# A fused HGRN2 and GLA trunk on one core: slots ordered by time, casts of value jobs held in text order, evictions and weight sums moved in priority

## The chip, the cores and the metric

The kernel runs on one core of a Trainium2 chip. The metric is the device time of one execution in microseconds; the smaller, the better. All tensors are float32.

## The reference

One layer with two mixers in parallel on the same normalised input (1024 tokens, 1024 channels). All features come out of one projection; both mixers are gated linear attention, the HGRN2 one with 8 heads of 128 by 128, the GLA one with 4 heads of 128 keys by 256 values:

```python
h = rms_norm(x, norm_w[l]) * (1.0 + scale[:, None, :]) + shift[:, None, :]
proj = h @ w_in[l]
hq, hf, hi, hz, gq, gk, gv, gz, ga, mg = jnp.split(proj, IN_OFFSETS, axis=-1)
y_h = hgrn2_branch(hq, hf, hi, hz, lb_all[l], hgrn_norm_w[l])
y_g = gla_branch(gq, gk, gv, gz, ga, gla_alpha_w[l], gla_alpha_b[l], gla_norm_w[l])
u_h = y_h @ w_branch[l, 0]
u_g = y_g @ w_branch[l, 1]
mg = jax.nn.sigmoid(mg.reshape(B, T, N_BRANCH, D_MODEL))
merged = mg[:, :, 0] * u_h + mg[:, :, 1] * u_g
x = x + gate[:, None, :] * (merged @ w_out[l])
return rms_norm(x, final_norm_w)
```

Each head computes, token by token, `S_t = diag(alpha_t) S_(t-1) + k_t v_t^T` and `o_t = S_t^T q_t`; the kernel does it in chunks.

## The kernel before

**Products.** A float32 factor is held as a rounded part and a rest: ScalarE casts it (L200), VectorE subtracts the cast from it (L201), both in `split`. Three matmuls (high by high, high by low, low by high) make one product. The large products are moreover done in seven products of halves in place of eight (Strassen's way), so that sums and differences of quarters of the factors have to be built: `make_factor` (L1691) and `v_sums` for the activations and the value weights, `weight_sums` (L1156 to L1162) for the gate and branch weights, which VectorE adds and POOL stores to DRAM for later.

**Stages in time.** The first group (matmuls L375, banks emptied by L351) makes normalised queries and keys of GLA. Value stage 0, from about 110 us, makes GLA's values: `Vstage`, matmuls L1852. Then come features of GLA (`Feat`, L583), value stage 1 (HGRN's values, about 348 to 464 us), the features of the HGRN heads (L583), and the last stages: branches and gates (L1304) and the output product (L1481).

**A value stage** has 14 jobs (`Vjob`): seven products in the order 1, 2, 5, 3, 6, 7, 4, each of two parts of the inner dimension (`kk`). A job is four units, one for each of four PSUM banks; a unit is six matmuls of 128 by 512. After the second part of a product each bank is emptied by `Vstage.after`: ScalarE copies it out for products 1 (L1737), 2, 5, 3 and 4 (L1735), and after 3 writes a snapshot back into the bank (L1755); VectorE combines it with a snapshot after 6 (L1759) and 7 (L1763). POOL stores results as v (L1742). The next product's matmuls on that bank wait for this. `prep` makes a job's splits, `load` its loads.

**Beside the jobs** run side tracks. `Stream.go` lets a job issue a unit and calls `weave`, which counts units and lets the heads' `attention` and the weights' sums go on: each is a generator whose `yield n` says how many units to let pass first. A head multiplies queries and decays (L633 to L637), makes scores (matmuls L641, L672), copies them on ScalarE (L692, L750 to L756), transposes keys (L767, copied by L768), makes states (L787) and outputs (L806, L808). GLA's outputs go through L972, L973, L980 and a norm (L949, L950), are multiplied in L987 and stored as yg by POOL (L877).

**Order.** Each engine works through its instructions in a fixed order. A list scheduler sets it when the kernel is built: it follows the order of the text, lets what it takes to be ready go ahead, and `tc.high_priority(offset=n)` makes an instruction count as standing n instructions further up. `tc.keep_in_program_order` holds instructions so marked in the order of the text among themselves.

**Slots.** Work tiles of 4 KB per partition live in 46 slots of SBUF. `Slots.get` takes the free slot with the smallest key; a tile written into it waits until the last readers of the former one are done, be it an engine or a store. `Slots.free` gives the number of tiles taken so far as the key, plus `behind` where the last reader is a store by DMA; `behind` is 0 until the last stages, then 8.

## Time and profile before

| | |
|---|---|
| time, three runs | 1219.4, 1222.74, 1224.36 us; median 1222.74 |
| profiled execution | 1223.05 us, of it the span 1221.3 us |
| TensorE busy, its mean granted clock | 1172.3 us, 96% of the span; 0.991 |
| VectorE, ScalarE, POOL busy | 848.1, 586.3, 123.4 us |

The span runs from the first to the last instruction. In a row of the timeline stand the start, the duration, engine, line, operation, the tiles written and read, and in brackets how long the engine had idled before and what ended this. A group of equal instructions in a row has its count behind the x. A row of the view of waits names the waiting instruction, what it waited for, then the total time, the number of times and the longest one. PEclk is TensorE's granted clock as a share of full speed.

### The profile page before, as it was taken

The page shows a single profiled execution, that of the slowest core. Times are in us where ns is not written, and L with a number is a line of the kernel's source. Part 1 is how long each engine was busy: PE and PEld are TensorE (multiplying, and loading weights), DVE is VectorE, ACT ScalarE, POOL GpSimd, SP SyncE. Part 2 cuts the span into 40 slices and gives each one's busy share as a digit, 9 for nine tenths or more (in the row PEclk, how much of TensorE's full clock was granted, in tenths as well). Part 3 has the DMA queues.
Part 4 walks back from the last instruction along what each step waited for, and adds up shares of the span by engine and source line. Part 5 has one row for each costly group of instructions (what it writes and reads, how often), then busy time and mean ns, then how long its engine had stood idle before and what let it go on. Part 6 is the DMA issues. An engine that isn't in the chain of part 4 may idle for free.

```text
span 1221.3 us, 20302 instructions
## 1 busy us (share of the span) xinstructions
PE 1172.3 (96%) x8137; PEld 954.2 (78%) x8137; DVE 848.1 (69%) x1270; ACT 586.3 (48%) x859; POOL 123.4 (10%) x256
## 2 busy tenths in 40 slices
PE   7999999999998899899999999999999999999997
PEld 5776767788877778688887888888878888878886
DVE  4745766776564766676877895876454765988994
ACT  5674454643453635243343344356544544544554
POOL 4211101010100012111111000000020000000000
PEclk9999999999999999899999999999999999999999
DMA  9764545384734568652835642234798856434433
GB/s 327 249 222 147 200 138 156 122 289 127 240 106 172 171 197 295 200 170 99 251 110 160 198 120 82 95 114 153 241 327 276 264 159 211 153 104 169 162 102 138
DMA packets 150353, 220.19 MB, mean 180 GB/s; under 512 B 8939, under 2 KB 107297, under 8 KB 150258
## 3 DMA queue, kind: packets, MB, share of 16 engines
q1 hardware_dynamic: 131970, 157.84, 41.5%
q0 software_dynamic: 18240, 61.04, 13.1%
q8 instruction: 64, 1.05, 0.4%
q14 instruction: 31, 0.25, 0.1%
q10 hardware_dynamic: 48, 0.01, 0.0%
HBM read 153.84 MB, written 65.01 MB: 179 GB/s over the span
## 4 chain that ended last, share of the span: by engine, by line
issue 50%; PE 32%; POOL 5%; DMA 5%; DVE 3%; ACT 2%; SPq 0%; POOLq 0%; DVEq 0%; ACTq 0%
PE pd L1304 9%; PE sc_ps L1304 5%; PE pm L1304 5%; PE pd L1852 3%; PE pd L1481 3%; DMA b<-in_w_in_dram 3%; POOL ws L1162 2%; PE sc_ps L1481 2%; PE pm L1481 1%; PE pd L583 1%; DMA v<-b 1%; PE pd L375 1%; POOL yh L877 1%; DVE b L201 1%; DMA b<-in_x_dram 1%
## 5 line engine op out<-in xcount | busy, mean ns | idle before, releaser
L583 PE MATMUL pd<-b,b 128*128 128x512 f32 x1632 | 390.3, 395 | 0.0
L583 PEld LDWEIGHTS pd<-b,b 128*128 128x128 f32 x1632 | 302.5, 188 | 64.6 <-issue 0.7
L201 DVE TENSOR_TENSOR b<-b,b 128x1024 fp32r<-128x1024 f32 (+1 forms) x114 | 129.6, 1148 | 78.3 <-ACT b L200 52.0
L1852 PE MATMUL pd<-b,b 128*128 128x512 f32 x672 | 167.7, 404 | 12.1 <-ACT b L1735 4.1
L1304 PE MATMUL pd<-b,b 128*128 128x512 f32 x720 | 173.0, 391 | 0.9 <-DVE b L1396 0.4
L200 ACT CAST b<-b 128x1024 fp32r<-128x1024 f32 (+1 forms) x114 | 111.0, 989 | 123.4 <-DMA b<-in_w_in_dram 39.3
L1852 PEld LDWEIGHTS pd<-b,b 128*128 128x128 f32 x672 | 125.7, 191 | 45.5 <-ACT b L1735 5.9
L1304 PEld LDWEIGHTS pd<-b,b 128*128 128x128 f32 x720 | 134.0, 188 | 31.2 <-DVE b L1396 0.9
L1247 DVE TENSOR_TENSOR b<-b,b 128x1024 fp32r<-128x1024 f32 x56 | 68.2, 1222 | 69.1 <-ACT b L1246 49.1
L1246 ACT CAST b<-b 128x1024 fp32r<-128x1024 f32 x56 | 58.6, 1051 | 68.1 <-PE pm L1304 19.4
L1304 PE MATMUL sc_ps<-b,b 128*128 128x512 f32 x324 | 78.6, 390 | 0.0
L1304 PE MATMUL pm<-b,b 128*128 128x512 f32 x300 | 72.1, 389 | 0.0
L1304 PEld LDWEIGHTS sc_ps<-b,b 128*128 128x128 f32 x324 | 60.4, 188 | 13.3 <-ACT b L1276 0.4
L1224 DVE TENSOR_TENSOR b<-b,b 128x1024 fp32r<-128x1024 f32 x48 | 57.8, 1220 | 16.9 <-ACT b L1223 11.2
L1223 ACT CAST b<-b 128x1024 fp32r<-128x1024 f32 x48 | 49.8, 1050 | 39.9 <-PE pd L1304 15.9
L1304 PEld LDWEIGHTS pm<-b,b 128*128 128x128 f32 x300 | 56.3, 188 | 11.7
L1162 POOL DMA_DIRECT2D ws<-b x64 | 34.7, 542 | 216.4 <-DVE b L1156 83.9
L375 PE MATMUL pd<-b,b 128*128 128x512 f32 x192 | 52.3, 405 | 3.6 <-DVE b L351 2.7
L692 ACT COPY xb<-b 128x512 f32<-128x512 f32 x48 | 29.4, 619 | 43.5 <-PE sc_ps L672 27.3
L375 PEld LDWEIGHTS pd<-b,b 128*128 128x128 f32 x192 | 34.4, 188 | 16.2 <-DVE b L351 3.5
L806 PE MATMUL pm<-scT,b 128*128 128x128 f32 x256 | 46.8, 275 | 0.0
L808 PE MATMUL pm<-b,b 128*128 128x128 f32 x224 | 43.3, 275 | 0.0
(313 smaller groups left out, 1627.4 us busy)
## 6 DMA issues: line engine op xcount, KB each, us to landing
b<-in_w_in_dram SPq DMA_DIRECT2D x72, 512.0 KB, 4.8
ws<-b POOLq DMA_DIRECT2D x64, 256.0 KB, 3.4
b<-ws SPq DMA_DIRECT2D x32, 512.0 KB, 4.8
b<-in_x_dram SPq DMA_DIRECT2D x16, 512.0 KB, 5.9
b<-in_ada_w_dram SPq DMA_DIRECT2D x32, 256.0 KB, 6.4
v<-b POOLq DMA_DIRECT2D x32, 256.0 KB, 3.1
b<-v SPq DMA_DIRECT2D x16, 512.0 KB, 4.6
b<-fx SPq DMA_DIRECT2D x16, 512.0 KB, 4.1
```

What stands on the lines that cost most here:

```text
L200: nc.scalar.copy(hi, src)
L201: nc.vector.tensor_sub(lo, src, hi.bitcast(F32))
L375: nc.tensor.matmul(accs[f], wg(a, d, f), b[d][:, half * 512:half * 512 + 512], start=(d == 0 and n == 0), stop=(d == KT - 1 and n == 2))
L583: nc.tensor.matmul(ps[0:w, th * 512:(th + 1) * 512], a[:, k, 0:w], b[:, th * 512:(th + 1) * 512], start=(k == 0 and n == 0), stop=(k == KT ...
L1162: nc.gpsimd.dma_start(w_sums[b][i // 2][q][:, i % 2 * 512:i % 2 * 512 + 512], parts[p].rearrange("p k f -> p (k f)"))
L1223: nc.scalar.copy(hi, src)
L1224: nc.vector.tensor_sub(lo, src, hi.bitcast(F32))
L1246: nc.scalar.copy(hi, t)
L1247: nc.vector.tensor_sub(lo, t, hi.bitcast(F32))
L1304: nc.tensor.matmul(o, a[:, sl], c, start=(p in (1, 5) and kt == 0 and n == 0), stop=(kt == 3 and n == 2), skip_group_check=True)
L1481: nc.tensor.matmul(o, a, b, start=(p in (1, 5) and kt == 0 and n == 0), stop=(kt == 3 and n == 2), skip_group_check=True)
L1852: nc.tensor.matmul(st.bank[i], x_, w_, start=(p in (1, 5) and kk == 0 and a == 0 and n == 0), stop=(kk == 1 and a == 1 and n == 2), skip_g ...
```

## The change

- `Slots`: the key of a freed slot is the number of units issued so far (`S.now`, from `weave`; plus 2 for each run of the output product), and `behind` is 4 from the start to the end.
- `pinned_split` is used by the value jobs: its casts keep the order of the text.
- `Vstage.after` runs with an offset of 300 (`EVICT_FIRST`), the four adds of `weight_sums` with one of −400 (`BEHIND`).
- `Stream.go` loads up to two jobs more at the start of a job whose `more` is set, and prepares one job less at its unit 0.
- Head 0's query and key are loaded at the start of job 10 of value stage 0, and no longer at job 12.
- In `attention`, the wait after the score copies is 3 units (was 3.5), the one behind the transposes 2.5 (was 1.5).

```diff
--- before.py
+++ after.py
@@ -25,6 +25,7 @@
 C_HQ, C_HF, C_HI, C_HZ = 0, 1024, 2048, 3072
 C_GQ, C_GK, C_GV, C_GZ, C_GA, C_MG = 4096, 4608, 5120, 6144, 7168, 7184
 N_SLOTS = 46
+EVICT_FIRST, BEHIND = 300, -400
 PACE, PACE_H = 1.08, 1.15
 
 
@@ -39,7 +40,8 @@
     def __init__(self, pool, n):
         self.pool = pool
         self.free_list = [(-1, i - n, i) for i in range(n)]
-        self.freed = self.behind = 0
+        self.freed = self.now = 0
+        self.behind = 4
         self.owner = {}
         self.serial = 0
 
@@ -53,7 +55,7 @@
     def free(self, *tiles, sent=False):
         for t in tiles:
             self.freed += 1
-            heapq.heappush(self.free_list, (self.serial + (self.behind if sent else 0), self.freed, self.owner.pop(id(t))[0]))
+            heapq.heappush(self.free_list, (self.now + (self.behind if sent else 0), self.freed, self.owner.pop(id(t))[0]))
 
 
 class Halves:
@@ -198,6 +200,12 @@
             hi = S.get(list(src.shape[1:]), F32R)
             lo = S.get(list(src.shape[1:]), F32R)
         nc.scalar.copy(hi, src)
+        nc.vector.tensor_sub(lo, src, hi.bitcast(F32))
+        return hi, lo
+
+    def pinned_split(src):
+        hi, lo = S.get([2, 512], F32R), S.get([2, 512], F32R)
+        tc.keep_in_program_order(nc.scalar.copy(hi, src))
         nc.vector.tensor_sub(lo, src, hi.bitcast(F32))
         return hi, lo
 
@@ -755,7 +763,7 @@
         for j in range(4):
             nc.scalar.copy(scT[32 * j:32 * j + 32, :, 32 * j:32 * j + 32], blk[32 * j:32 * j + 32])
         scoring.discard(me)
-        yield 3.5
+        yield 3
 
 
         kT = S.get([NCH, P])
@@ -767,7 +775,7 @@
                 nc.tensor.transpose(pt[:, i * P:(i + 1) * P], k[:, ch * P:(ch + 1) * P], ident)
             nc.scalar.copy(kT[:, g * 4:g * 4 + nt, :].rearrange("p c s -> p (c s)"), pt[:, 0:nt * P])
         S.free(k)
-        yield 1.5
+        yield 2.5
         per = 512 // V
         spp = 1024 // V
         st = [S.get([1024]) for _ in range((7 + spp - 1) // spp)]
@@ -842,16 +850,17 @@
         def go(self, loads=2, preps=1):
             n = len(self.jobs)
             for i, job in enumerate(self.jobs):
-                self.ahead(i, loads, 0)
+                self.ahead(i, loads + 2 * job.more, 0)
                 for u, _ in enumerate(job.run()):
                     if job.calls(u):
-                        self.ahead(i, loads + 2 * job.more, preps + job.more)
+                        self.ahead(i, loads + 2 * job.more, preps + (job.more if u else 0))
                     if (n - i, u) in self.hooks:
                         self.hooks[n - i, u]()
                     self.weave(1)
 
         def weave(self, units):
             self.units += units
+            S.now = self.units
             for track in (self.side, self.back):
                 if not track:
                     continue
@@ -1153,11 +1162,13 @@
         s1, s2 = S.get([2, 4, P]), S.get([2, 4, P])
         parts = {5: s1[:, 0], 6: s1[:, 1], 3: s2[:, 0], 7: s2[:, 1]}
         add = nc.vector.tensor_add
-        add(parts[7], x1[:, :, 0], x1[:, :, 1])
-        add(parts[5], x1[:, :, 1], x2[:, :, 1])
+        with tc.high_priority(offset=BEHIND):
+            add(parts[7], x1[:, :, 0], x1[:, :, 1])
+            add(parts[5], x1[:, :, 1], x2[:, :, 1])
         yield 1.5
-        add(parts[6], parts[7], x2[:, :, 1])
-        add(parts[3], parts[6], x2[:, :, 0])
+        with tc.high_priority(offset=BEHIND):
+            add(parts[6], parts[7], x2[:, :, 1])
+            add(parts[3], parts[6], x2[:, :, 0])
         for p, q in SUMS.items():
             nc.gpsimd.dma_start(w_sums[b][i // 2][q][:, i % 2 * 512:i % 2 * 512 + 512],
                                 parts[p].rearrange("p k f -> p (k f)"))
@@ -1563,6 +1574,7 @@
         for p in OUT_PRODUCTS:
             for i in range(4):
                 out_run(p, i)
+                S.now += 2
                 out_after(p, i)
                 for f in at.get((4, p, i), ()):
                     f()
@@ -1799,10 +1811,10 @@
             s, p, kk = self.stage.s, self.p, self.kk
             add = nc.vector.tensor_add
             if s:
-                self.w = split(self.w_raw)
+                self.w = pinned_split(self.w_raw)
                 S.free(self.w_raw)
                 if p not in RAW_X:
-                    self.x = split(self.x_raw)
+                    self.x = pinned_split(self.x_raw)
                     S.free(self.x_raw)
                 return
             if p == 2:
@@ -1815,7 +1827,7 @@
                 add(wq[0, 1][kk], wq[0, 0][kk], wq[1, 1][kk])
                 nc.vector.scalar_tensor_tensor(wq[1, 0][kk], wq[0, 1][kk], -1.0, wq[1, 0][kk], ALU.mult, ALU.subtract)
             raw = wq[W_AT[p]][kk]
-            self.w = split(raw)
+            self.w = pinned_split(raw)
             if p in (3, 6, 7, 4):
                 S.free(raw)
             if p == 3:
@@ -1826,7 +1838,7 @@
                 S.free(xq["22"][kk], sent=True)
             if p not in RAW_X:
                 x = xq[QUAD[p]][kk]
-                self.x = split(x)
+                self.x = pinned_split(x)
                 if p in (7, 4):
                     S.free(x, sent=True)
 
@@ -1852,7 +1864,8 @@
                         nc.tensor.matmul(st.bank[i], x_, w_, start=(p in (1, 5) and kk == 0 and a == 0 and n == 0),
                                          stop=(kk == 1 and a == 1 and n == 2), skip_group_check=True)
                 if kk:
-                    st.after(p, i)
+                    with tc.high_priority(offset=EVICT_FIRST):
+                        st.after(p, i)
                 yield
             S.free(*self.w)
             if p not in RAW_X:
@@ -1864,9 +1877,9 @@
     vjobs = [[Vjob(st, p, kk) for p in PRODUCTS for kk in range(2)] for st in (Vstage(0), Vstage(1))]
 
     def first_head():
-        load_qk(0)
         start_side(gla_attention(0))
 
+    vjobs[0][10].begins = lambda: load_qk(0)
     vjobs[0][12].begins = first_head
 
     def pause(on):
@@ -1910,7 +1923,6 @@
     front()
     stream.go()
     S.free(*h_hi, *h_lo)
-    S.behind = 8
     lent = [dtile() for _ in range(2)]
     R.lend([pd[:, i * 512:i * 512 + 512] for pd in lent[::-1] for i in range(2)])
     last_stages()
```

The new lines move the numbers: what is L201 in `split` is L203 there, L1735 is L1747, L1759 is L1771, L1763 is L1775, L633 to L637 are L641 to L645, L972 is L981; the cast and the subtract of `pinned_split` are L208 and L209. The names b_n are numbered work tiles, pd_n PSUM banks, xb the buffer of a head's multiplied queries.

**VectorE, end of value stage 0**, between the last row that combines product 6 (L1759) and the first that empties a bank after product 7 (L1763); L634 is the first step of GLA head 0. Before:

```order
L1759 SCALAR_TENSOR_TENSOR b_1421<-pd_1129,b_1421 128x512
L201 TENSOR_TENSOR b_1565<-b_1325,b_1564 128x1024
L634 TENSOR_TENSOR xb<-b_1592,b_862 128x32x8
L635 TENSOR_TENSOR xb<-b_1592,b_862 128x32x8x2
L201 TENSOR_TENSOR b_1561<-b_1141,b_1560 128x1024
L636 TENSOR_TENSOR xb<-xb,b_862 128x32x16
L201 TENSOR_TENSOR b_1605<-b_1522,b_1604 128x1024
L1763 TENSOR_TENSOR b_1322<-pd_1128,b_1322 128x512
L637 TENSOR_TENSOR xb<-xb,b_862 128x32x8
```

and with the change:

```order
L1771 SCALAR_TENSOR_TENSOR b_1421<-pd_1137,b_1421 128x512
L209 TENSOR_TENSOR b_1541<-b_1132,b_1540 128x1024
L209 TENSOR_TENSOR b_1545<-b_1316,b_1544 128x1024
L643 TENSOR_TENSOR xb<-b_1518,b_862 128x32x8x2
L209 TENSOR_TENSOR b_1581<-b_1133,b_1580 128x1024
L209 TENSOR_TENSOR b_1585<-b_1317,b_1584 128x1024
L644 TENSOR_TENSOR xb<-xb,b_862 128x32x16
L203 TENSOR_TENSOR b_1622<-b_1516,b_1621 128x1024
L1775 TENSOR_TENSOR b_1326<-pd_1136,b_1326 128x512
L1775 TENSOR_TENSOR b_1349<-pd_1137,b_1349 128x512
```

Between the two stood three subtracts, now there are five; L634 (now L642) has gone ahead of the last L1759, and the second eviction follows the first one directly.

**ScalarE, value stage 1, end of product 5**: L972 reads outputs of a GLA head, L633 starts the next head, L1735 copies a bank out. Before:

```order
L972 ACTIVATE b_3319<-pm_3311 128x512
L633 COPY xb<-b_3351 128x32x32
L972 ACTIVATE b_3319<-pm_3322 128x512
L200 CAST b_3366<-b_3238 128x1024
L200 CAST b_3377<-b_3274 128x1024
L200 CAST b_3417<-b_3303 128x1024
L1735 COPY b_3360<-pd_3001 128x512 x2
L1735 COPY b_3387<-pd_3002 128x512
```

and with the change:

```order
L981 ACTIVATE b_3321<-pm_3313 128x512
L981 ACTIVATE b_3321<-pm_3324 128x512
L208 CAST b_3341<-b_3175 128x1024
L202 CAST b_3373<-b_3274 128x1024
L1747 COPY b_3361<-pd_3007 128x512
L641 COPY xb<-b_3363 128x32x32
L1747 COPY b_3361<-pd_3007 128x512
L1747 COPY b_3383<-pd_3008 128x512
```

The second L972 of the pair came after L633 and is now ahead of it; three casts stood ahead of the first L1735, two do now, and L633 has gone behind it.

**ScalarE, ahead of the first HGRN head**, whose decay comes from L1061 and L1062 (now L1070 and L1071); the casts of b_4263 and b_4385 are those of two feature weights. Before (the two rows that follow are L1061 and L1062):

```order
L200 CAST b_4486<-b_4263 128x1024
L200 CAST b_4026<-b_3930 128x1024
L951 ACT_TABLE_LOAD
L951 ACTIVATE b_3970<-pm_4036,eps_t 128x512
L951 ACTIVATE b_3970<-pm_4040,eps_t 128x512
L200 CAST b_4348<-b_4146 128x1024
L952 ACT_TABLE_LOAD
L952 ACTIVATE b_3970<-b_3970 128x1024
L937 ACT_TABLE_LOAD
L937 ACTIVATE b_4065<-pd_3984 128x1024
L633 COPY xb<-b_4065 128x32x32
L200 CAST b_4611<-b_4385 128x1024
```

and with the change:

```order
L961 ACTIVATE b_3977<-b_3977 128x1024
L946 ACT_TABLE_LOAD
L946 ACTIVATE b_4065<-pd_3962 128x1024
L641 COPY xb<-b_4065 128x32x32
L202 CAST b_4486<-b_4263 128x1024
L202 CAST b_4609<-b_4385 128x1024
L1070 ACTIVATE b_4139<-pd_4068 128x1024
L1071 ACTIVATE b_4140<-pd_4068 128x1024
L673 COPY xb<-b_4065 128x64x4
```

The cast of b_4263 stood far up, ahead of the norm's L951, and now stands with that of b_4385 directly ahead of the decay.

## The prediction

> **What bounds the kernel now.** I read the totals first, then what TensorE waited for, then the granted clock around its longest waits, then the rows of the engines that it waited for.
>
> ```profile
> core 0: 1221.3 us, clock 0.991
> PE 1172.3 (96%) x8137; PEld 954.2 (78%) x8137; DVE 848.1 (69%) x1270; ACT 586.3 (48%) x859; POOL 123.4 (10%) x256
> ```
>
> TensorE is the bound. The change takes no matmul away, so it can only gain idle TensorE time (1221.3 − 1172.3 = 49 us), and matmuls that ran at a lower clock. The view of waits, TensorE's alone, says who ended that idle time (total, times, longest, in us):
>
> ```profile
> PE sc_ps L641 <- DVE xb L637: 5.8, 1, 5.8
> PE pm L787 <- ACT b L768: 5.5, 6, 1.3
> PE pd L1852 <- ACT b L1735: 4.1, 3, 3.7
> PE pd L1852 <- DVE b L1763: 2.9, 1, 2.9
> PE pd L375 <- DVE b L351: 2.7, 2, 1.5
> PE pd L1852 <- ACT b L1737: 1.7, 2, 1.5
> PE pd L1852 <- DVE b L1759: 1.7, 1, 1.7
> PE pd L1852 <- ACT pd L1755: 1.4, 1, 1.4
> PE pm L950 <- DVE b L201: 1.3, 1, 1.3
> ```
>
> The rows of L1852 are a value stage's matmuls that wait until a PSUM bank has been emptied: 4.1 + 2.9 + 1.7 + 1.7 + 1.4 = 11.8 us. The others wait for a step of an attention head, of the GLA norm, or of the first group. Three waits are long (5.8, 3.7, 2.9 us), and behind each of them the windows show the clock down (window, length, busy us by engine, then PEclk):
>
> ```profile
> 182.80:190.00 7.20, 7.17 (x41) 5.33 (x42) 5.96 (x9) 0.00 (x0) 1.63 (x3) 0.57 0.29 109
> 396.90:402.00 5.10, 5.04 (x15) 4.02 (x16) 4.29 (x7) 2.23 (x4) 0.00 (x0) 0.67 0.30 103
> 506.30:512.00 5.70, 5.70 (x76) 4.88 (x77) 5.70 (x11) 1.96 (x3) 1.23 (x3) 0.69 0.37 141
> 426.60:432.00 5.40, 4.39 (x111) 3.42 (x112) 5.40 (x15) 1.86 (x3) 0.94 (x2) 1.00 0.33 106
> ```
>
> Lost clock is (1 − PEclk) times the length: 7.2 × 0.43 = 3.1, 5.1 × 0.33 = 1.7, 5.7 × 0.31 = 1.8 us. The last row follows the 1.7 us wait, and its clock is full: short waits cost only themselves, long ones 1.7 to 3.1 us more.
>
> The Trainium skill ("TensorE: Matmul & The Clock Gate", Part 1 and "Why this matters for your kernels") has the clock fall after an idle window of about 3.4 us and tells to avoid gaps above some 3 us. The 2.89 us gap here was followed by 0.57; the measurement decides. By the page's figure alone that gap would carry no clock loss, and place A below would be an estimated 3.1 us smaller.
>
> **Part by part.** No instruction of a compute engine is added. The edits cost what their new order costs; I go through the places where TensorE waits now.
>
> *A, 182.83 us (value stage 0, product 7 to 4).*
>
> ```profile
> 172.04 0.68 DVE L1759 SCALAR_TENSOR_TENSOR b<-pd,b 128x512 f32<-128x512 f32 x1
> 173.10 1.23 DVE L201 TENSOR_TENSOR b<-b,b 128x1024 fp32r<-128x1024 f32 x1 [0.38 <-ACT b L200]
> 176.56 0.66 DVE L634 TENSOR_TENSOR xb<-b,b 128x256 f32<-128x256 f32 x1 [2.23 <-DMA b<-qk]
> 179.05 1.22 DVE L201 TENSOR_TENSOR b<-b,b 128x1024 fp32r<-128x1024 f32 x1 [1.07 <-DMA v<-b]
> 182.08 0.69 DVE L1763 TENSOR_TENSOR b<-pd,b 128x512 f32<-128x512 f32 x1
> 182.83 1.65 PE L1852 MATMUL pd<-b,b 128*128 128x512 f32 x3 [2.89 <-DVE b L1763]
> ```
>
> VectorE is in order: L1763, which frees the bank, stood behind L634, which waited 2.23 us for head 0's query load, and behind a subtract L201 that waited 1.07 us for a store out of its slot. The query load now starts two jobs earlier, and slots just stored are taken four units later, so I strike both waits. But the order puts two more L201 ahead of L1763 (five instead of three after the last L1759; L634 now stands earlier). From 172.04 to the end of L1763 (182.08 + 0.69) are 10.7 us, of which 0.38 + 2.23 + 1.07 = 3.7 are waits and 7.0 work. Less 0.6 for L634 and plus two L201 of 1.2 less a little overlap, that is 8.7, so L1763 ends near 180.7. TensorE ran dry at 182.83 − 2.89 = 179.94: 0.8 us stay. Gain 2.1, and 3.1 of clock: **5.2**. If the loads don't come earlier, the two L201 make it worse by 2.3.
>
> *B, 396.96 us (value stage 1, product 5 to 3).*
>
> ```profile
> 386.67 6.55 PE L1852 MATMUL pd<-b,b 128*128 128x512 f32 x28
> 388.76 1.23 DVE L201 TENSOR_TENSOR b<-b,b 128x1024 fp32r<-128x1024 f32 x1 [6.86 <-DMA v<-b]
> 388.06 1.05 ACT L633 COPY xb<-b 128x1024 f32<-128x1024 f32 x1 [2.61 <-DMA b<-qk]
> 394.29 2.13 ACT L200 CAST b<-b 128x1024 fp32r<-128x1024 f32 x2 [3.75 <-issue]
> 396.33 0.58 ACT L1735 COPY b<-pd 128x512 f32<-128x512 f32 x1
> ```
>
> L201 waited 6.86 us for a store of v; behind it stood L973 and L980 (the gated GLA sum), whose result the first of the two casts at 394.29 needs, and behind these ScalarE's L1735. In the new order all L972 stand together ahead of L633, L980 comes before the subtracts, and L1735 follows one cast after it, with L633 behind. ScalarE is free at 388.06 − 2.61 = 385.5; one L972, the last L973 and L980, two casts and L1735 take about 0.6 + 0.7 + 1.2 + 2.1 + 0.6 = 5.2: it ends near 390.7, against 393.2, where TensorE ran dry. The wait goes: 3.7 + 1.7 = **5.4**, with 2.5 us to spare.
>
> *C, the short waits of value stage 1.*
>
> ```profile
> 360.54 1.64 ACT L756 COPY scT<-blk 32x256 f32<-32x256 f32 x4
> 362.20 1.09 ACT L1737 ACTIVATE b<-pd 128x512 f32<-128x512 f32 x2
> 411.88 1.04 ACT L200 CAST b<-b 128x1024 fp32r<-128x1024 f32 x1
> 412.83 0.59 ACT L1755 COPY pd<-b 128x512 f32<-128x512 f32 x1
> ```
>
> L1737 stood behind a head's score copies, L1755 behind a cast, L1759 behind score steps of the same kind. All three now stand further ahead. L1755 gains the cast (0.95 of 1.4 us), L1737 and L1759 most of 1.5 and 1.7. What is put back are score steps of a head, each 0.2 to 1 us: TensorE's next score matmuls come that much later, so I take 3.5 of 4.6: **3.5**.
>
> *D, 506.30 us (first HGRN head).*
>
> ```profile
> SPq L565 <- DMA yg<-b: 10.6, 1, 10.6
> 491.82 0.37 SPq L565 DMA_DIRECT2D b<-in_w_in_dram  x1
> 477.20 23.32 PE L583 MATMUL pd<-b,b 128*128 128x512 f32 x102
> 497.60 1.05 ACT L200 CAST b<-b 128x1024 fp32r<-128x1024 f32 x1 [10.06 <-DMA b<-in_w_in_dram]
> 499.47 1.02 ACT L1062 ACTIVATE b<-pd 128x1024 f32<-128x1024 f32 x1
> 505.52 0.64 DVE L637 TENSOR_TENSOR xb<-xb,b 128x256 f32<-128x256 f32 x1
> ```
>
> A weight load was held 10.6 us on SP, because its slot was still being stored as yg; its cast stood 10.06 us on ScalarE, ahead of L1061 and L1062, which the head's first scores need. TensorE was dry from 500.5. In the new order that load gets a slot that no store reads. Yet the cast ahead of it, formerly done by 480, now has a slot of yg, so ScalarE still waits for this store, until about 491.6 (the old load was issued at 491.82, when it landed) or, if the gate sums ahead of L987 wait for their own, earlier queued loads, up to 1.5 us longer. Two casts, L1061 and L1062 take 4 us; the two adds L1156 and L1157 that stood between L634 and L637 (0.6 each) are gone. From L1062 on 505.52 + 0.64 − 499.47 = 6.7 us remain, less 1.2. L1062 starts near 494.7 to 496.2, L637 ends near 500.2 to 501.7. I take 501.7, a rest of 1.2: gain 4.6 + 1.8 = **6.4**.
>
> *E, the end of the first group*: a loss.
>
> ```profile
> 111.16 1.23 DVE L1691 TENSOR_TENSOR b<-b,b 128x1024 f32<-128x1024 f32 x1 [1.03 <-DMA b<-h]
> ```
>
> L1691 and a subtract come ahead of two L351, which free banks of the first group. One such row more in the way is 1.2 us; the casts that wait for these L1691 come earlier instead. I book **−0.8**, between +0 and −2.4 with the clock kept.
>
> *F, the rest.* L950 waited 1.3 us for L201, with a subtract and an add ahead that the new order puts behind: **1.3**. Of the six waits of L787, two heads' follow an add that waited for its load ahead of the score steps; the row of one is
>
> ```profile
> 659.82 0.75 DVE L1033 TENSOR_SCALAR b<-b,cs 128x1024 f32<-128x1024 f32 x1 [2.48 <-DMA b<-in_ada_w_dram]
> ```
>
> In those two heads the add has moved: **2.3** for both. The other yields move L767 six matmuls up and leave L787 in place: nothing, since L787 waits for L768, which stands behind ScalarE's score copies. Behind 850 us the engines' orders agree: nothing.
>
> Sum of gains: 5.2 + 5.4 + 3.5 + 6.4 − 0.8 + 1.3 + 2.3 = 23.3 us. Against it stand **new waits**: nearly every tile has another slot, and SP's loads of the weights' sums have changed places. Nothing in the trace prices these; bounds are 0 and two long waits of A's kind, 2 × (2.9 + 3.1) = 12. Short waits are the commoner row, so I take three of 1.5: 4.5. The profiled execution took 1223.05 us (1.75 around the span), 0.3 above the median of 1222.74. 1223.05 − 23.3 + 4.5 = 1204.3, less 0.3 for the median: **1204 us**.
>
> **The rivals.**
>
> *1. Everything works and no new wait comes.* 1222.74 − 23.3 = 1199; with the other L787 waits (3.2 us) gone too, 1196. For it: B has 2.5 us to spare. Against it: A and D are close to their limits.
>
> *2. The waits move.* What was behind the evictions gets late instead. One long wait with its clock loss stays or appears (A or D: 5 to 6 us), C gains half: 1204 + 6 + 2 = 1212, and with a second one 1218. For it: at A five L201 stand where three did, and at D a yg slot is still in the way.
>
> *3. The orders barely change what is waited for.* The offsets move only instructions whose neighbours are within 300 or 400 of text, and DVE's rows for GLA heads read alike in both orders. Then only B's reorder counts and E takes back some: 1219 to 1223.
>
> *4. Slower: pinned casts hold ScalarE.* A cast kept in text order waits for its own load with all evictions behind it.
>
> ```profile
> ACT b L200 <- DMA b<-in_w_in_dram: 39.3, 9, 10.1
> ```
>
> Casts already wait 39.3 us for weight loads, up to 10.1 at once. If a value stage's products meet this, each costs what B costs now, 5.4 us. With D and F still gained (10) and A, B, C lost, three such waits make 1222.7 − 10 + 16.2 = 1229: from three on the change is slower. Against it: a stage's loads run at least two ahead, so most casts have their data.
>
> The store's landing decides much in all of these.
>
> ```profile
> v<-b POOLq DMA_DIRECT2D x32, 256.0 KB, 3.1
> ```
>
> A unit is six matmuls, 6 × 6.55 / 28 = 1.4 us, so four units are 5.6 us against a landing of 3.1: late only where POOL itself is. The Trainium skill ("SBUF — State Buffer", section "SBUF: two separate sides") lets VectorE's two-port work starve the descriptors of POOL's transfers, which speaks against slots that wait for stores while VectorE is made busier. With VectorE busy 69% the row shows 3.1 us at the median, so it bears out no such starving here; by the rule a store can stretch by a VectorE instruction, an estimated 1 us, within the four units.
>
> **How the numbers follow.** Forecast (1199 to 1211) 0.55; rival 1 0.12; rival 2 0.18, half of it above 1216.6; rival 3 0.08; rival 4 0.07. A measurement of this kernel tells about 0.5%, 6.1 us, from no change: faster is below 1216.6, slower above 1228.9. Faster: 0.55 + 0.12 + 0.09 = 0.76, with one point of rival 3 0.77; same 0.16; slower 0.07. Leaving out the better part of rival 1, and rivals 3 and 4, the range is 1196 to 1219.
>
> **What would show it.** Right: no TensorE wait for L1735 or L1763 above 1.5 us, the clock 1.00 at 182 to 190 and 397 to 402, the wait of L641 under 2 us, two waits of L787 fewer, and a span near 1202. A: L634 without a wait for qk; B: no L201 waiting for v for 6 us; D: the cast ahead of L1061 starting before 495. Wrong: a TensorE wait over 2.9 us for L351 near 108, or at a place that has none now; or ScalarE's L200 waiting for weight loads in the value stages.

## The result, and the profile after

The changed kernel takes 1217.3 us at the median (eight runs, 1211.31 to 1218.46) against 1222.67 us for the kernel before (eight runs beside it, 1219.4 to 1224.36): a ratio of 0.9955, 95% interval 0.994 to 0.9969. The change is 5.4 us faster, a quarter to a third of the 18.7 us that were forecast: inside the stated range, outside the likeliest case's own. It is also less than the 0.5% (6.1 us) that the prediction took for what a measurement tells from no change; with eight runs of each the interval still leaves 1 out.

In the text below, a line that the prediction calls L633 to L637 is L641 to L645 now, L787 is L795, L768 is L776, L351 and L375 are L359 and L383, L1691 is L1703, L891 and L897 are L900 and L906, L1735, L1759, L1763 and L1852 are L1747, L1771, L1775 and L1864, L1061 is L1070, and the casts and subtracts L200 and L201 are L202 and L203, or L208 and L209 where they are held.

The totals of the changed kernel's page (the profiled execution took 1218.36 us):

```profile
core 0: 1216.7 us, clock 0.988
PE 1173.9 (96%) x8137; PEld 956.0 (79%) x8137; DVE 846.7 (70%) x1270; ACT 584.0 (48%) x859; POOL 122.9 (10%) x256
```

TensorE idles 42.8 us (1216.7 − 1173.9), 6.2 us less than before, but it is busy 1.6 us longer with the same 8137 matmuls, and its mean clock is lower: 0.988 for 0.991 (the eight runs go from 0.987 to 0.993). So in this execution some of the idle time that went was paid back at a lower clock. TensorE's waits (total in us, times, longest; left out are those of the first 25 us, which every kernel here has, up to 3.5 us long, and most of the short ones):

```profile
PE pm L795 <- ACT b L776: 9.2, 5, 5.2
PE pd L383 <- DVE b L359: 5.2, 1, 5.2
PE sc_ps L649 <- DVE xb L645: 4.8, 1, 4.8
PE pm L775 <- ACT b L922: 2.7, 1, 2.7
PE pd L1864 <- ACT b L1747: 1.7, 4, 1.1
PE pd L1864 <- ACT b L1749: 0.9, 2, 0.6
PE pd L1864 <- DVE b L1771: 0.3, 1, 0.3
```

The value stages' waits for banks are 1.7 + 0.9 + 0.3 = 2.9 us, where they were 11.8. But four waits of 2.7 to 5.2 us stand where before there were three: one in the first group (at 113 us), one at a GLA head's transposes (221 us), the old one at the first HGRN head (494 us), and one at a head's states (660 us). The windows behind these four, and one at place B in value stage 1 (window, length, busy us by engine, then PEclk):

```profile
113.10:121.00 7.90, 7.89 (x22) 5.66 (x23) 5.72 (x7) 2.24 (x3) 2.71 (x5) 0.68 0.45 168
220.80:228.00 7.20, 7.14 (x27) 6.03 (x28) 4.64 (x7) 7.11 (x9) 0.00 (x0) 0.78 0.00 0
494.20:502.00 7.80, 7.73 (x80) 6.47 (x81) 7.66 (x14) 1.95 (x3) 0.00 (x0) 0.60 0.25 69
660.10:668.00 7.90, 7.83 (x34) 6.99 (x35) 4.24 (x11) 1.69 (x4) 1.62 (x3) 0.74 0.39 111
395.00:402.00 7.00, 6.38 (x27) 5.08 (x28) 6.07 (x9) 6.94 (x10) 0.00 (x0) 1.00 0.40 150
```

Lost clock in this execution, worked out as in the prediction, is 7.9 × 0.32 + 7.2 × 0.22 + 7.8 × 0.40 + 7.9 × 0.26 = 2.5 + 1.6 + 3.1 + 2.1 = 9.3 us; the three places of before lost 6.6. At B the clock is full.

Where the time went is seen best by the **lead**: how much earlier the trace of after has done the same amount of matmul work than that of before (where the matmuls stand in one order, how much earlier the same matmul starts). Its changes from place to place add up to the 4.6 us between the two spans:

| stretch | lead at its end, us | change | forecast |
|---|---|---|---|
| to 93 us | 0.7 | +0.7 | 0 |
| first group's end (E) | −4.4 | −5.1 | −0.8 |
| value stage 0 (A) | 1.2 | +5.6 | 5.2 |
| transposes at 221 us | 0 | −1.2 | 0 |
| value stage 1 (B and C) | 9.5 | +9.5 | 8.9 |
| GLA norm at 476 us (L950) | 11.1 | +1.6 | 1.3 |
| first HGRN head (D) | 10.8 | −0.3 | 6.4 |
| HGRN heads to 629 us | 9.6 | −1.2 | 0 |
| heads at 664 to 694 us | 4.0 | −5.6 | 1.2 (half of F) |
| heads to 782 us | 6.6 | +2.6 | 1.2 (half of F) |
| the rest | 4.6 | −2.0 | 0 |

The value stages gave what was forecast and a little more. The loss lies at E, D and 660 us, and a smaller one at 221 us. The rows of the timeline there (start, duration, engine, line, tiles; in brackets the idle time before) show these three causes. At E, VectorE and TensorE:

```profile
103.35 1.23 DVE L1703 TENSOR_TENSOR b<-b,b 128x1024 f32<-128x1024 f32 x1 [4.14 <-DMA h<-b]
...
110.09 1.23 DVE L906 TENSOR_TENSOR b<-b,b 128x1024 f32<-128x1024 f32 x1 [3.64 <-ACT b L904]
...
113.11 1.65 PE L383 MATMUL pd<-b,b 128*128 128x512 f32 x3 [5.23 <-DVE b L359]
```

The difference L1703 writes over a tile that POOL stores as h. The store was issued at 94.72 us and took 8.5 us to land (issue to landing), and L1703, which was ordered ahead of the key's normalisation, waited for it with VectorE standing still. Behind it came L900, L901, ScalarE's answer, L906 (3.5 us later than the L897 of before, at 106.56), and only then the L359 that frees the bank. At D, the store of yg, the casts behind it on ScalarE, and the end of the chain on VectorE:

```profile
477.27 2.13 POOL L886 DMA_DIRECT2D yg<-b  x4
...
484.18 2.00 ACT L202 CAST b<-b 128x1024 fp32r<-128x1024 f32 x2 [5.75 <-DMA yg<-b]
...
493.49 0.64 DVE L645 TENSOR_TENSOR xb<-xb,b 128x256 f32<-128x256 f32 x1
```

TensorE was dry here from 494.3 − 4.8 = 489.5 us on, 11 us earlier than before (500.5). The casts began once the store had landed, at 484.2, and only some 7.5 us earlier than that landing before (about 491.8, when the load that waited for it was issued). And at 660 us, on ScalarE:

```profile
653.31 2.00 ACT L202 CAST b<-b 128x1024 fp32r<-128x1024 f32 x2 [7.25 <-DMA ws<-b]
...
659.53 0.97 ACT L776 COPY b<-pm 128x512 f32<-128x512 f32 x2
```

The casts of a later feature's weight stand ahead of what the running head needs, up to the copy of its transposed keys (L776), and wait 7.25 us for a slot out of which a weights' sum is still being stored.

### The profile page after: what moved, and what is told of

It is laid out like the page before. It is cut to its first block, busy times and chain, and to the rows that moved or that the text cites. A ratio compares the mean times of both kernels' runs of the same rounds, so it can differ in the third digit from the quotient of the medians.

```text
span 1216.7 us, 20300 instructions
## 1 busy us (share of the span) xinstructions
PE 1173.9 (96%) x8137; PEld 956.0 (79%) x8137; DVE 846.7 (70%) x1270; ACT 584.0 (48%) x859; POOL 122.9 (10%) x256
## 4 chain that ended last, share of the span: by engine, by line
PE 48%; issue 35%; DMA 5%; DVE 4%; POOL 4%; ACT 2%; SPq 1%; POOLq 0%; DVEq 0%; ACTq 0%
PE pd L1315 10%; PE pd L591 8%; PE pd L1864 8%; PE pm L1315 5%; PE sc_ps L1315 5%; PE pd L1492 3%; DMA b<-in_ada_w_dram 2%; POOL ws L1173 2%; PE pd L383 2%; PE sc_ps L1492 2%; PE pm L1492 1%; DVE b L209 1%; PE pm L814 1%; PE sc_ps L383 1%; PE pm L816 1%
## 5 line engine op out<-in xcount | busy, mean ns | idle before, releaser
L1864 PE MATMUL pd<-b,b 128*128 128x512 f32 x672 | 164.1, 398 | 3.0 <-ACT b L1747 1.7
L1864 PEld LDWEIGHTS pd<-b,b 128*128 128x128 f32 x672 | 123.8, 188 | 36.9 <-ACT b L1747 4.9
L1258 DVE TENSOR_TENSOR b<-b,b 128x1024 fp32r<-128x1024 f32 x56 | 68.3, 1223 | 69.8 <-ACT b L1257 56.9
L202 ACT CAST b<-b 128x1024 fp32r<-128x1024 f32 (+1 forms) x70 | 65.9, 951 | 80.0 <-DMA b<-in_w_in_dram 22.9
L203 DVE TENSOR_TENSOR b<-b,b 128x1024 fp32r<-128x1024 f32 (+1 forms) x70 | 76.7, 1101 | 36.7 <-ACT b L202 35.8
L1257 ACT CAST b<-b 128x1024 fp32r<-128x1024 f32 x56 | 58.4, 1049 | 66.3 <-PE pm L1315 17.6
L209 DVE TENSOR_TENSOR b<-b,b 128x1024 fp32r<-128x1024 f32 x44 | 52.7, 1225 | 35.8 <-ACT b L208 34.2
L1235 DVE TENSOR_TENSOR b<-b,b 128x1024 fp32r<-128x1024 f32 x48 | 57.8, 1222 | 19.7 <-ACT b L1234 13.9
L1234 ACT CAST b<-b 128x1024 fp32r<-128x1024 f32 x48 | 49.7, 1049 | 44.9 <-PE pd L1315 15.5
L700 ACT COPY xb<-b 128x512 f32<-128x512 f32 x48 | 29.2, 619 | 62.4 <-PE sc_ps L680 36.4
L383 PE MATMUL pd<-b,b 128*128 128x512 f32 x192 | 52.8, 408 | 6.0 <-DVE b L359 5.2
L383 PEld LDWEIGHTS pd<-b,b 128*128 128x128 f32 x192 | 34.8, 190 | 18.7 <-DVE b L359 6.1
L208 ACT CAST b<-b 128x1024 fp32r<-128x1024 f32 x44 | 44.3, 1050 | 6.8 <-PE pd L1864 3.5
```

The costliest lines, as they stand in the source:

```text
L202: nc.scalar.copy(hi, src)
L203: nc.vector.tensor_sub(lo, src, hi.bitcast(F32))
L209: nc.vector.tensor_sub(lo, src, hi.bitcast(F32))
L383: nc.tensor.matmul(accs[f], wg(a, d, f), b[d][:, half * 512:half * 512 + 512], start=(d == 0 and n == 0), stop=(d == KT - 1 and n == 2))
L1235: nc.vector.tensor_sub(lo, src, hi.bitcast(F32))
L1257: nc.scalar.copy(hi, t)
```

## The experiments

Each ratio is against runs of the kernel before on the same chip, whose median went from 1218.35 to 1222.67 us between chips; so ratios are compared, not times. Two theories stood at the start. **Theory one:** the gain in the value stages comes from the changed slots and the earlier query load, as forecast, and what is lost comes from equal keys in the front stage (E), the offset of the weights' sums (660 us) and the two yields (221 us). **Theory two:** the held casts and the evictions' offset make the gain, and the slots are of no use or do harm.

| kernel | edit | ratio [95%] | its median; before beside it |
|---|---|---|---|
| after_again | the change, once more | 0.996 [0.9941, 0.9978] | 1216.79; 1220.59 |
| before_again | the kernel before, once more | 0.9995 [0.9986, 1.0005] | 1220.18; 1220.18 |
| u_evict | no offset for evictions | 0.9993 [0.9979, 1.0006] | 1218.42; 1219.35 |
| u_behind | no offset for sums | 0.9976 [0.9963, 0.9989] | 1215.88; 1219.35 |
| u_yields | old yields | 0.9958 [0.9941, 0.9974] | 1213.91; 1219.35 |
| u_slots | slot keys as before | 0.993 [0.99, 0.9959] | 1213.36; 1220.59 |
| u_pin | value casts not held | 1.0038 [1.0017, 1.0059] | 1227.37; 1220.59 |
| u_ahead | `Stream.go` as before | 0.9999 [0.9985, 1.0013] | 1220.62; 1220.44 |
| u_qk | query load at job 12 | 0.9986 [0.9974, 0.9998] | 1218.67; 1220.18 |
| f_front | old keys in the front stage only | 0.9964 [0.9948, 0.9981] | 1213.71; 1219.35 |
| x_allpin | feature casts held too | 0.9924 [0.9907, 0.9941] | 1210.35; 1218.35 |
| c_fy | f_front and old yields | 0.9916 [0.9884, 0.9948] | 1212.53; 1220.59 |
| c_fyp | c_fy, feature casts held | 0.9945 [0.9931, 0.996] | 1212.56; 1218.35 |
| c_syp | old keys, old yields, feature casts held | 0.9897 [0.988, 0.9915] | 1206.83; 1218.35 |
| c_sypb | c_syp, no offset for sums | 0.9882 [0.9867, 0.9897] | 1205.19; 1220.18 |
| pin_alone | before, value casts held | 1.0043 [1.0027, 1.0058] | 1223.89; 1218.35 |
| pin_qk | pin_alone, query load at job 10 | 1.0024 [1.0011, 1.0037] | 1222.74; 1220.18 |
| b_allpin | pin_qk, feature casts held | 0.9935 [0.9913, 0.9956] | 1213.53; 1220.44 |

### Both kernels once more

> The changed kernel as it is, on the same chip as the runs beside it, as their base line. A ratio of 0.9955 to the kernel before was measured for it; the same is expected here, within 0.002.

> The kernel before as it is, for a trace of it on the chip of these runs: the ratio is 1 within 0.002. Expected: the same three long waits as in the trace read for the prediction (183, 397 and 506 us); if one of them is below 1.5 us here, the chips differ in it and what the change gained there is less than the first trace says.

The second trace of the change has the same four waits (4.5, 2.7, 4.4 and 4.7 us), that of the kernel before the same three (2.1, 3.5 and 5.9). The waits belong to the kernels, not to one execution. The clock behind them doesn't: at A in the second trace of the kernel before, the clock was 0.75 over 6.7 us, a loss of 1.7 us where the first one lost 3.1.

### The front stage's keys (E)

```diff
-    heapq.heappush(self.free_list, (self.now + (self.behind if sent else 0), ...
+    key = self.serial - 10000 if self.front else self.now + (self.behind if sent else 0)
+    heapq.heappush(self.free_list, (key, ...
...
     front()
+    S.front = False
```

> The changed kernel, but until the front stage ends a freed slot's key is the number of tiles taken (as before the change), since no unit is counted there and all keys are equal; after it, the change's keys. My theory: equal keys gave the activation loads of value stage 0 their slots 20 us earlier, so the differences were put ahead of the gate's steps on VectorE and held them 4.1 us: the 5.2 us wait near 113 us with 2.5 us of clock. With this edit that place is as before (1.2 + 1.5 us, full clock): 1211 to 1213 us, unless the other slots of stage 0 bring new waits. Rival, the earlier preparation of jobs did it: the 5.2 us stay, 1217.

While the front stage runs, no unit is counted, so all its freed slots have the key 0 or 4; here they have the number of tiles taken, as before. VectorE at E, and TensorE's waits, in this kernel (its lines are two further down):

```profile
101.13 0.69 DVE L902 TENSOR_SCALAR b<-b 128x1024 f32<-128x1024 f32 x1 [4.44 <-ACT b L900]
...
106.74 1.23 DVE L908 TENSOR_TENSOR b<-b,b 128x1024 f32<-128x1024 f32 x1 [3.65 <-ACT b L906]
```

```profile
PE pm L797 <- ACT b L778: 8.7, 5, 5.1
PE sc_ps L651 <- DVE xb L647: 5.0, 1, 5.0
PE pd L385 <- DVE b L361: 2.8, 2, 1.8
```

L906's counterpart is back at 106.7 us, the wait for L361 at 1.8. With the old keys the loads of h wait for their slots until 108 us (86.4 in the change); so the differences are not ready early, and the scheduler leaves them behind the normalisation. The cause of E is shown. But the gain does not stay in this trace. Its lead over that of after_again is some 4 us at 123 us, 3.2 at 183 and at 483, 1.9 at 543, 0.3 at 723 and 0 at the end. Most of it goes at the first HGRN head and at 660 us. These are the windows of f_front, then those of after_again:

```profile
491.80:499.80 8.00, 7.99 (x81) 6.67 (x82) 7.83 (x15) 1.95 (x3) 0.00 (x0) 0.62 0.24 68
656.80:664.80 8.00, 7.94 (x32) 7.00 (x33) 4.01 (x10) 1.42 (x4) 1.63 (x3) 0.69 0.39 112
```

```profile
494.40:502.40 8.00, 7.94 (x87) 6.70 (x88) 7.83 (x15) 1.96 (x3) 0.00 (x0) 0.79 0.24 68
658.70:666.70 8.00, 8.00 (x39) 7.28 (x40) 4.79 (x11) 2.17 (x3) 1.62 (x3) 0.79 0.41 122
```

At the first head the wait is 0.6 us longer than in after_again (5.0 for 4.4), and the lost clock 1.4 us more (8.0 × 0.38 against 8.0 × 0.21); at 660 us it is 0.4 and 0.8. So the larger part went to the clock, and that this is the edit's doing is not shown: the last section has waits of equal length with very different losses. The traced execution (1216.1 us) is also the second slowest of six, whose median is 1213.71. Still, by the ratios (0.9964 for 0.9955 and 0.996) this edit gains nothing that can be told.

### The yields (221 us)

```diff
-        yield 3
+        yield 3.5
...
-        yield 2.5
+        yield 1.5
```

> The changed kernel with the two waits of attention as before (3.5 units behind the score copies, 1.5 behind the transposes). My theory: the transposes that come six matmuls earlier run into ScalarE's copies, which caused the 2.7 us wait near 221 us (2.2 before, in two pieces without a lower clock); with the old waits 1.3 + 0.9 come back in place of 2.7 + 1.6 of clock: 1214 to 1216 us. Rival, the split of the gate's matmuls beside it did it: the 2.7 us stay, 1217.

The wait at the transposes is back at its old size, and the clock behind it is full:

```profile
PE pm L775 <- ACT b L922: 1.3, 1, 1.3
```

```profile
220.80:228.00 7.20, 5.14 (x23) 4.09 (x24) 6.20 (x10) 7.09 (x9) 0.00 (x0) 1.00 0.11 31
```

The transposes six matmuls earlier came into ScalarE's score copies, behind which stands the L922 that frees their bank. This trace leads that of after_again by 2.15 us at its end, but the median ratio is that of the change: about 2 us in one execution, none that the runs can tell. The long wait at 660 us is not in this trace either (0.2 us there); one of 2.5 us stands at 611 us in its place, with a clock of 0.72 over the 6.2 us behind it.

### The wait at 660 us

```diff
-EVICT_FIRST, BEHIND = 300, -400
+EVICT_FIRST, BEHIND = 300, 0
```

> The changed kernel with BEHIND = 0: the adds of the weights' sums count at their own place again. My theory: the 5.2 us wait of the key products near 660 us (a cast on ScalarE that waits 7.3 us for a store of a weight sum out of its slot, the sum having been added late) comes from this offset; without it that wait falls to about 1 us and 2.1 us of clock come back: 1210 to 1212 us. Rival, the late load of the sum's factors did it, not the offset: a long wait for a store of a sum stays, 1216 to 1219.

```profile
PE pm L795 <- ACT b L776: 7.5, 5, 4.2
```

```profile
648.76 1.05 ACT L202 CAST b<-b 128x1024 fp32r<-128x1024 f32 x1 [5.75 <-DMA b<-in_w_in_dram]
```

The expectation fell: the wait stays at 4.2 us, with a cast ahead of the head's rows waiting 5.75 us for its load instead of for a store. What is common to both is that the cast stands ahead of the head's instructions. So the next kernel holds the features' casts in the order of the text too:

```diff
-        split(raw[:, :, 0:w], hi[:, :, 0:w], lo[:, :, 0:w])
+        tc.keep_in_program_order(nc.scalar.copy(hi[:, :, 0:w], raw[:, :, 0:w]))
+        nc.vector.tensor_sub(lo[:, :, 0:w], raw[:, :, 0:w], hi[:, :, 0:w].bitcast(F32))
```

> The changed kernel with the features' casts held in the order of the text too. Theory: the 5 us wait near 660 us comes from a feature's cast that the scheduler put ahead of an earlier one and of a head's copies, and that there waits for a store or a load out of its slot (7.3 us with the change, 5.8 us for a load without BEHIND); held in order it stands behind these copies, so the wait falls to about 1 us and its clock loss goes: 5 to 7 us below the changed kernel; the first head's wait near 494 us stays, since its casts were in order. Rival, the slot's wait moves with the cast and holds the next copies instead: within 2 us of the changed kernel.

TensorE's waits for the transposed keys, and ScalarE at the first HGRN head:

```profile
PE pm L796 <- ACT b L777: 9.4, 7, 2.2
```

```profile
477.95 1.02 ACT L1072 ACTIVATE b<-pd 128x1024 f32<-128x1024 f32 x1
478.85 1.06 ACT L580 CAST b<-b 128x1024 fp32r<-128x1024 f32 x1
```

The 5 us wait is gone; four of about 2 us take its place, and behind two of them the clock falls (0.72 over 6.2 us at 561, 0.71 over 5.8 us at 608). The wait at 221 us shrinks to 0.8. Unexpectedly the wait at the first HGRN head went as well (0.3 us): the cast that waited for the store of yg now stands behind the decays L1071 and L1072, which it had held up; the second of them runs at 477.95, and at 487.00 in the change. The waits at the first head and at 660 us were one thing, a feature's cast ahead of a head's work. The ratio, 0.9924, is the best of a single edit, though 0.993 of u_slots below can't be told from it.

### What the value stages' gain comes from

```diff
-                self.w = pinned_split(self.w_raw)
+                self.w = split(self.w_raw)
```

(and so for the other three splits of `Vjob.prep`)

> The changed kernel with split in place of pinned_split: the value jobs' casts may be moved by the scheduler again. Theory (the slots' keys made the gain): the value stages' waits stay below 4 us and the time within 2 us of the changed kernel's. Rival (the held casts made it): casts come again ahead of copies out of a bank, the waits at 396 and 413 us come back with 3.7 and 1.4 us, and the kernel is 5 us or more slower than the changed one.

TensorE's waits, and ScalarE's rows at 416 us, where the longest of them is:

```profile
PE pd L1864 <- ACT pd L1767: 6.0, 1, 6.0
PE pd L1864 <- ACT b L1747: 4.1, 4, 3.1
```

```profile
414.48 1.04 ACT L202 CAST b<-b 128x1024 fp32r<-128x1024 f32 x1 [4.71 <-issue]
...
415.91 1.11 ACT L1767 COPY pd<-b 128x512 f32<-128x512 f32 x2
```

A cast ahead of the write-back L1767 began only after 4.71 us, which TensorE spent idle; the profile names nothing that it waited for. The trace loses 11.6 us to after_again between 363 and 423 us, and the medians differ by 10.6. No other undo costs as much.

```diff
-        self.behind = 4
+        self.behind = 0
...
-    heapq.heappush(self.free_list, (self.now + ...
+    heapq.heappush(self.free_list, (self.serial + ...
...
+    S.behind = 8
     lent = [dtile() for _ in range(2)]
```

> The changed kernel with the slots' keys as before (number of tiles taken, nothing added for stores until the last stages), all else as changed. My theory now, as the kernel without EVICT_FIRST kept nearly all of the gain in the value stages: the keys made it, since a subtract or cast no longer lands in a slot that is still being stored. Then the waits for a store of v come back here and with them 3 to 4 us at the end of product 5 of stage 1 and 2 to 3 us at the end of product 7 of stage 0, each with its lower clock; the 5.2 us near 113 us fall to about 2.7. Sum: 3 to 7 us above the changed kernel. Rival, the held casts made it: the value stages stay short (below 4 us of waits in all) and the kernel is 4 to 6 us below the changed one, from 113 us alone.

```profile
PE pd L383 <- DVE b L359: 2.7, 2, 1.7
PE pd L1864 <- DVE b L1771: 1.8, 2, 1.2
PE pd L1864 <- ACT b L1747: 1.5, 3, 0.8
```

E is back at 1.7 us, and B, which the prediction put on the slots, stays at 0.8 with the old keys. All waits for banks of the value stages are 7.1 us, 4.2 more than in the change, though each is short; 4.4 of them are in stage 0, where f_front, which differs in the keys behind the front stage alone, has 1.3 and gains 2.4 us on this kernel by 195 us (by the lead). So the new keys do help in stage 0. The long wait at 660 us is not there. At 0.993 against 0.996 the new keys cost some 3 us over the whole kernel, if anything (the intervals overlap), and neither theory nor rival of this run is borne out whole.

```diff
-                self.ahead(i, loads + 2 * job.more, 0)
+                self.ahead(i, loads, 0)
...
-                        self.ahead(i, loads + 2 * job.more, preps + (job.more if u else 0))
+                        self.ahead(i, loads + 2 * job.more, preps + job.more)
```

> The changed kernel with Stream.go as before. Theory: this edit is what the held casts need, since it takes one job's preparation out of unit 0, where the evictions of the product before are due; without it the value stages' waits rise by 3 us or more (2.9 with the change) and the ratio is 0.998 or more, as for the held casts with the query load alone (1.0024). Rival, it does nothing by itself: 0.995 to 0.997, the value stages as in the changed kernel.

```profile
PE pd L1864 <- ACT b L1747: 2.9, 3, 2.4
```

Its 2.4 us stand at 396.6, place B: without this edit part of B's wait is back, and the change loses about 5 us by the ratios (2.75 between the two traces).

```diff
-    vjobs[0][10].begins = lambda: load_qk(0)
     def first_head():
+        load_qk(0)
```

> The changed kernel with the query and key load back at job 12. Theory: without the earlier load the held casts bring a wait of 3 us or more at the end of product 7 of stage 0 (0.2 us with the change), with 2 to 3 us of clock: 4 to 7 us slower than the changed kernel. Rival, the slots by time get the load in time anyway: within 2 us.

```profile
PE pd L1864 <- DVE b L1775: 2.6, 1, 2.6
```

The 2.6 us are place A again, at 187.5: without the earlier load the change loses 3.8 us by the ratio to its first run (0.9955), 3.2 by that to after_again, a little less than expected.

```diff
-EVICT_FIRST, BEHIND = 300, -400
+EVICT_FIRST, BEHIND = 0, -400
```

> The changed kernel with EVICT_FIRST = 0: what empties a value stage's bank counts at its own place again, all else as changed. My theory: this offset removed most of the waits of value stage matmuls (11.8 us before, 2.9 after). Without it they come back, at least at the end of product 7 of stage 0 (2.9 us and some 3 of clock) and in stage 1 (4 to 9 us): 1222 to 1228 us, against 1217.3 of the change. Rival, the slots alone did it (the waits for a store of v are gone without the offset too): 1216 to 1219, the value stages' waits below 4 us.

By the ratios this loses 4 to 4.6 us, and the intervals do not meet. The trace doesn't show where: the waits for banks are 3.3 us where the change has 2.9, and the lead over after_again is −1.8 us. This is open.

Neither of the two theories stands whole. The held casts carry the gain at B, the earlier query load that at A, and the keys by time help in stage 0; the loss at E is that of equal keys; and the one at 660 us comes from where a feature's cast stands, not from the offset of the sums.

### Holding casts without the rest

```diff
+    def pinned_split(src):
...
-                self.w = split(self.w_raw)
+                self.w = pinned_split(self.w_raw)
```

(in the kernel before, for all four splits)

> The kernel before with one edit of the change alone: the value jobs' casts held in the order of the text. Theory now: holding them is what gained, since it keeps a later job's casts from going ahead of a copy out of a bank: the waits of value stage matmuls fall from 11.8 us to below 6, the clock losses at 183 and 397 us go at least in part, and the time falls by 5 to 9 us. Rival, the casts must be held together with slots that no store reads: the waits for a store of v stay on ScalarE and VectorE, with casts held in order behind them, and the gain is below 3 us.

TensorE's wait at 188 us, and VectorE's there:

```profile
PE pd L1858 <- DVE b L1769: 4.6, 1, 4.6
```

```profile
181.83 0.66 DVE L640 TENSOR_TENSOR xb<-b,b 128x256 f32<-128x256 f32 x1 [4.66 <-DMA b<-qk]
```

B falls from 3.7 to 0.6 us and the waits for banks at 413 and 426 are gone (in their stead one of 2.1 us for the copy after product 1, at 367, and one of a head's scores, 2.2 us at 428), and yet the kernel is slower than before: place A has got 4.6 us, since the first step of the head (L640) waits for its query load that much longer with the evictions behind it. The next kernel takes the query load forward as well.

```diff
+    vjobs[0][10].begins = lambda: load_qk(0)
```

> The kernel before with two parts of the change: the casts held, and head 0's query and key loaded two jobs earlier. Theory: held alone, the casts let VectorE's L640 (L634 before) wait 4.7 us for that load ahead of the eviction at 188 us; with the load earlier that wait of 4.6 us falls below 1 with its clock loss, and the kernel is 4 to 8 us faster than with the held casts alone (which was 1.0043 of the kernel before): 0.997 to 1.000. Rival, the subtracts in front of the eviction are the limit: the wait stays above 2.5 us, ratio above 1.001.

```profile
PE pd L1858 <- ACT b L1741: 3.7, 4, 2.8
```

The wait at 188 us goes, as it should; but 2.8 us are back at B, with 2.05 at 362 and 2.2 at 428, and the ratio is the rival's. Nothing is gained by these two parts alone.

```diff
+        tc.keep_in_program_order(nc.scalar.copy(hi[:, :, 0:w], raw[:, :, 0:w]))
```

(the features' casts, on top of pin_qk)

> The kernel before with the value and the feature casts held and the query load two jobs earlier. Theory: the features' casts are what waits ahead of the first HGRN head (5.8 us at 506 us) and of key copies later; held, these waits fall by 4 to 6 us with 1 to 3 of clock, on top of 1.0024 without them: 0.994 to 0.998. Rival, the first head's casts wait for the store of yg wherever they stand: above 1.000.

```profile
PE sc_ps L648 <- DVE xb L644: 2.8, 1, 2.8
```

With all casts held the first HGRN head waits 2.8 us in place of 5.8, and 1.0024 becomes 0.9935. Holding all casts and the earlier query load, without new keys, offsets, yields or `Stream.go`'s edit, come to as much as the whole change or a little more (the intervals overlap).

### The parts that work, together

These kernels join edits whose diffs stand above.

> The changed kernel with two edits that each took a long wait away: keys by tiles taken until the front stage ends, and the old waits in attention. Theory, the losses have separate causes and add: at 113 us about 2.8 us of waits with full clock (5.2 + 2.5 with the change), at 221 us 2.2 (2.7 + 1.6), near 655 us no wait above 2.5: 6 to 9 us below the changed kernel. Rival, each new order puts a long wait somewhere by chance: the sum of the waits stays that of the single edits, and the time within 2 us of them.

Old keys in the front stage and old yields: 4.3 us below the change on the same chip, less than the 6 to 9 expected, and no wait of an HGRN head above 2.5 us. The traced execution has a clock of 0.997, the other three 0.992 and 0.993. Its lead over after_again is only 1.1 us at 475 us and 5.1 at the end, made at the first HGRN head and at 660 us, where no long wait is left.

> The changed kernel with three edits: keys by tiles taken until the front stage ends, the old waits in attention, and the features' casts held. Without the last one 1212.5 us were measured (0.9916 of the kernel before), with waits of 2.5 us near 609 and 2.2 near 491. Theory: the held casts take away what is left of waits behind feature casts, 2 to 4 us: 1208 to 1211. Rival, they now stand late and the features' matmuls wait for them: 1213 or more.

A miss: with held feature casts on top it is no better, and a wait for transposed keys of 3.6 us stands at 513 us. Why the edit that helps the change by some 4 us does not help here is open.

> The changed kernel with the slots' keys wholly as before, the old waits in attention, and the features' casts held: no slot rule left, the holding and the offsets alone. Theory: the keys cost more than they gave (without them the change was 3.5 us faster), so this is within 2 us of the version with keys by time behind the front stage, 1208 to 1212. Rival, keys by time are needed where stores are dense, at product 5 of stage 1 and the first head: the waits there are 3 us or more, 1213 to 1217.

Old keys all through, old yields, all casts held: 1206.83 us, faster than expected. It differs from c_fyp in the keys behind the front stage alone, ran on the same chip, and is 5.7 us faster, with intervals that do not meet: here the keys by time cost more than they give. By the lead they do give in the value stages: c_syp is 6.4 us behind c_fyp at 455 us, 2.4 ahead at 635 and 3.9 ahead at the end. The gain lies at the HGRN heads, c_fyp's wait at 513 us among it.

> The version with slots' keys as before, old waits in attention and all casts held (0.9897 of the kernel before), with BEHIND = 0 as well. Theory: the offset of the sums has little effect (without it alone the changed kernel was 0.9976 against 0.996): within 0.002 of 0.9897. Rival, late sums keep slots taken that the first head's casts need: the 3 us wait at 493 us falls below 1.5 and the ratio is 0.987 or less.

The totals, waits and one window of this kernel:

```profile
PE 1165.7 (97%) x8137; PEld 949.0 (79%) x8137; DVE 847.9 (71%) x1270; ACT 583.7 (49%) x859; POOL 122.8 (10%) x256
```

```profile
PE pm L796 <- ACT b L777: 3.8, 9, 1.0
PE sc_ps L650 <- DVE xb L646: 3.0, 1, 3.0
```

```profile
490.00:498.00 8.00, 8.00 (x77) 6.43 (x68) 7.97 (x15) 1.96 (x3) 1.62 (x3) 0.80 0.61 197
```

This is the fastest kernel: 1205.19 against 1220.18 us for the kernel before, ratio 0.9882 [0.9867, 0.9897], 15 us. TensorE idles 36.4 us of a span of 1202.1, and its matmuls take 8.2 us less than in the change. Behind the first 25 us one wait of 3 us is left, at the first HGRN head, with a clock of 0.80 behind it. Whether the offset of the sums helps or harms can't be told: 0.9897 with it, 0.9882 without, and the intervals overlap.

## Why the prediction was right and wrong

**A, B, C and L950 were right in size, and wrong in part on the cause.** Forecast 5.2 + 5.4 + 3.5 + 1.3 = 15.4, measured +5.6, +9.5 (B and C) and +1.6. At A the query load was the right cause (u_qk brings the wait back). At B the prediction had L201's wait for a store of v, and so the slots, as what held the casts and L1735 back. With the old slot keys B stays short (u_slots), while without held casts 10.6 us are lost (u_pin) and without `Stream.go`'s edit B's wait returns (u_ahead). It is the places of the casts, not the slots' ages, that decided B. A's 3.1 us of clock were one execution's (1.7 in before_again), so that its sum came out has some luck in it.

**E was booked at −0.8 and cost 5.1.** The step that failed is "one such row more in the way is 1.2 us". Rows were counted by their own duration. But the row put in the way has a wait of its own: 4.14 us, for a store of its tile. All of the chain behind it came later, and TensorE's wait grew to 5.2 us with 2.5 us of clock. f_front shows why the row came there: equal keys let the loads of h start 20 us earlier.

**D was booked at +6.4 and gave nothing.** The step that failed is the comparison of the new chain with TensorE's old arrival. The chain did end earlier than forecast (L645 at 494.1, forecast 500.2 to 501.7), but "TensorE was dry from 500.5" had become 489.5 by the gains of A, B and C, while the store of yg, and with it the cast ahead of the decays, came only 7.5 us earlier. The difference of 3.5 us is what is missing between the forecast rest (1.2) and the wait (4.8). The prediction had named the cast that still waits for this store, and not drawn the conclusion that a gain ahead of it is lost there as far as the store does not come earlier too. D and E together (6.7 and 4.3) are some 11 of the 13.3 us that are missing from the forecast of 18.7.

**F was half right.** One of the two waits that were struck is gone (+2.6 before 782 us); at the other head a cast with a 7.25 us wait took the place of the add that was moved. x_allpin shows that this cast's place is the cause, and u_behind that the offset is not. The lead fell by 5.6 us there.

**The yields were booked at nothing** and show 1.2 us at 221 in the trace; undoing them moves the wait and its clock, but not the median.

**The allowance for new waits** of 4.5 us took short ones to be commoner. The new one at 660 is long, 5.2 + 2.1 us with its clock, and the one at 221 grew to 2.7 + 1.6. Rival 2 (the waits move, one or two long ones with their clock, 1212 to 1218) is nearest to what happened, though C gained in full. The prediction's own signs of being wrong came: 5.2 us for L359 at 113, and a long wait at a place that had none. Rival 4 was the reverse of the truth for this change, in which the held casts are the best part; yet in the kernel before they alone do cost time (pin_alone), by a wait for a load ahead of evictions, as that rival has it, only on VectorE.

Not settled: where u_evict loses its time, why c_fyp gains nothing over c_fy, the sign of the sums' offset, and what decides how much clock a wait costs.

## What to carry to other kernels

On engines that run in order, look at what stands ahead of an eviction or of a head's steps, and ask whether that row itself waits for a load or a store: a row that is cheap by its duration can hold up everything behind it by a DMA's landing. When several gains are added up, go down the timeline with the new arrival times, for a wait that ends with a DMA takes back what was gained ahead of it as far as the DMA does not move as well (here 11 us met a store that came 7.5 us earlier). And try each part of a bundle by itself: here holding the order of all casts was worth more than the new allocation of slots, which helped in the value stages and cost more behind them.
